# A planner that counts bank reads and stores, and an earlier first stage, in a hybrid gMLP and neighbourhood-attention block

## The chip, the cores and the metric

One core of a Trainium2 chip. The metric is device time in microseconds (us); lower is better.

## The reference

```python
S, D_MODEL, CHUNK, A_WIDTH, A_GROUPS = 2048, 1024, 128, 512, 4
B_HEADS, B_HEAD_DIM, GRID_W, WIN_ROWS_MAX, WIN_COLS, D_FF = 8, 64, 64, 8, 16, 4096
h = rms_norm(x, norm1_g)
proj = h @ w_in                                  # [u, v | q, k, av | gates a, b]
z_a = gelu(proj[..., :1024])
y_a = u * (einsum('gpq,bnqgc->bnpgc', w_s, layer_norm(v)) + b_s)
q, k = rms_norm(q, q_g) * hd ** -0.5, rms_norm(k, k_g)
y_b = attention of each of 32 x 64 grid cells over its 8 x 16 window, with bias rpb
gates = sigmoid(gate_pre + b_gate)               # 2 x 1024 columns
merged = gates[..., :1024] * (y_a @ w_o_a) + gates[..., 1024:] * (y_b @ w_o_b)
x = x + merged @ w_out
x = x + square(relu(rms_norm(x, norm2_g) @ w_ff1)) @ w_ff2
```

All is float32.

## The kernel before

Every product is made of three TensorE products of a high and a low part (hi and lo of both operands, without lo by lo), each 128x128 by 128x512. The large products go by a seven-product scheme: a unit takes sums of four blocks of weights (w_r, w_s and their hi and lo parts r and t; `w_seven`, L1377) and of rows (r1, r2, t23, t4) and makes 7 x 12 = 84 products (`seven`, L1447). They run in the order 1, 5, 6, 3, 7, 2, 4 over three banks of PSUM, z, x and y. ScalarE copies bank z after product 1 and 6 and bank x after 5 (`feat`, L330), and the next product that adds to the bank waits for that copy. GpSimd makes the sums (`sums`, L352, for rows; L1391 to L1401 for weights), ScalarE casts them (L1351, L1435), VectorE subtracts for the low part (L1355, L1439).

The rows are two halves h of 1024 tokens. `first_steps` (L1012) goes: `first_u` (L419), which makes u of h 0 by 192 whole products on the rows as loaded, with the mean square from squares on GpSimd (L408) and additions on VectorE (L414); eight units of gates of h 0; two units of u of h 1; eight units of gates of h 1; then values and queries of all rows, by slices that they load from DRAM (xf, `x_slice`). Beside these, `rows_out` (L540) loads rows of xT, scales them (L556), sums them and stores them to xf: four jobs for h 1 in units 2 to 5 of the first gates, four for h 0 in the first four units of the second gates. `first_w` (L574) does the same for the weights of values and queries. `bias_tables` (L935) builds the attention's bias on GpSimd's own DMA queue: 24 loads, three masks and 93 puts (L989), spread over gates and u. Attention, merge, output product and two up and down stages of the MLP follow, by units of the same kind.

The order on every engine is fixed ahead by a planner (`Plan.run`, L112). A step is TensorE work with a cost; a chain is a list of stages on SP, ScalarE, VectorE or GpSimd, each with a cost, a lead before the step that needs it, and the count of buffers (51 in all) that it takes or gives back. A stage is issued at the latest at its due step, and earlier where its engine's clock and the buffers allow. All stages of a chain that are due are issued at once, ready or not (`force`, L180), and what an engine was given runs in that order.

```python
while k < len(c.stages) and c.latest[k] <= i:
    k += 1
if k > c.done:
    force(c, k, i, t0)
```

## Time and profile before

| | |
|---|---|
| median of 3 runs | 2709.9 us (2708.07 to 2717.45) |
| the profiled execution | 2714.44 us |
| its span | 2712.6 us |
| its mean granted TensorE clock | 0.972 |
| DMA | 573.76 MB, 211 GB/s over the span |

The page gives busy time by engine: PE is TensorE's products, PEld its weight loads, DVE VectorE, ACT ScalarE, POOL GpSimd, SP the engine that issues most DMAs. A view by windows gives the same for a stretch of time, with the granted clock and the DMA share. A timeline row shows start and duration of an instruction, `out<-in`, and in square brackets how long its engine sat idle before it and what ended that. In the view of waits, a row names who waited for whom: total, times, longest.

### The profile page before, as it was taken

What the parts mean: (1) busy time and instruction counts of PE and PEld (TensorE: products, weight loads), DVE (VectorE), ACT (ScalarE), POOL (GpSimd) and SP (SyncE); (2) the same over time, 40 slices, a digit from 0 to 9 for tenths busy, and PEclk for the clock granted to TensorE, in tenths of its full rate; (3) what the DMA queues carried; (4) which work ended last, traced back from release to release, by engine and by line L of the source; (5) the groups of instructions that cost most, each with busy time, mean ns of one, the idle gap of its engine ahead of it and who ended that gap; (6) DMA issues with size and microseconds to landing.
All of it is one profiled execution on the core that took longest, in us unless ns stands there. A gap on an engine that the chain in (4) does not pass through costs nothing.

```text
span 2712.6 us, 34217 instructions
## 1 busy us (share of the span) xinstructions
PE 2535.4 (93%) x11820; PEld 2063.4 (76%) x11820; DVE 1831.4 (68%) x2593; ACT 1185.2 (44%) x1854; POOL 1136.2 (42%) x904
## 2 busy tenths in 40 slices
PE   7689699899998999999998999899998999989999
PEld 6577578687776777778886888778886888868887
DVE  6756556777887666663646666687877566678876
ACT  4455344665554555532334443433334444434341
POOL 6756568100000111132435766533432676734341
PEclk9899899999999999999998999899999999989999
DMA  5578878878778999986865444654346444474443
GB/s 163 161 244 235 283 246 290 318 211 250 207 197 214 306 322 323 328 310 217 283 223 177 152 153 144 212 193 166 133 147 233 152 152 148 147 263 144 157 142 113
DMA packets 402844, 573.76 MB, mean 212 GB/s; under 512 B 34477, under 2 KB 269396, under 8 KB 402672
## 3 DMA queue, kind: packets, MB, share of 16 engines
q1 hardware_dynamic: 389888, 557.65, 63.6%
q0 software_dynamic: 8640, 13.92, 1.9%
q8 instruction: 93, 1.52, 0.2%
q10 hardware_dynamic: 4144, 0.02, 0.1%
q14 instruction: 79, 0.65, 0.1%
HBM read 368.45 MB, written 202.98 MB: 211 GB/s over the span
## 4 chain that ended last, share of the span: by engine, by line
PE 70%; DMA 11%; DVE 7%; issue 3%; POOL 3%; ACT 2%; SPq 1%; DVEq 0%; POOLq 0%; ACTq 0%
PE z L1467 28%; PE x L1467 13%; PE fg L304 11%; PE y L1467 7%; PE z L640 4%; PE x L640 2%; DMA vw<-vs 1%; PE y L640 1%; PE s L1154 1%; DMA w<-in_xT_dram 1%; PE pv L1226 1%; PE pTp L1199 1%; DMA kst<-ks 1%; DVE x_r L1439 1%; DMA bias<-tb 1%
## 5 line engine op out<-in xcount | busy, mean ns | idle before, releaser
L1467 PE MATMUL z<-x_t,t_hi 128*128 128x512 f32 x1184 | 376.1, 399 | 60.2 <-ACT fe L330 25.9
L1355 DVE TENSOR_TENSOR r_lo<-w_r,r_hi 128x1024 fp32r<-128x1024 f32 (+3 forms) x176 | 280.9, 1597 | 107.3 <-ACT r_hi L1351 102.8
L1394 POOL TENSOR_TENSOR w_s<-w_r 128x512 f32<-128x512 f32 (+3 forms) x88 | 152.6, 1734 | 396.0 <-DVE x L1784 164.4
L1467 PEld LDWEIGHTS z<-x_t,t_hi 128*128 128x128 f32 x1184 | 226.3, 193 | 115.0 <-ACT fe L330 27.6
L1101 POOL CAST q<-qn 128x256 fp32r<-128x256 f32 x128 | 48.7, 423 | 588.6 <-DMA ks<-qo 337.9
L1467 PE MATMUL z<-x_t,t_lo 128*128 128x512 f32 x592 | 234.7, 396 | 0.9 <-DVE t_lo L1355 0.9
L1351 ACT CAST r_hi<-w_r 128x1024 fp32r<-128x1024 f32 (+3 forms) x176 | 173.8, 989 | 123.1 <-PE z L1467 47.0
L1467 PE MATMUL x<-x_r,t_hl 128*128 128x512 f32 x888 | 218.5, 394 | 1.9 <-DVE t_hl L1355 1.9
L1467 PEld LDWEIGHTS x<-x_r,t_hl 128*128 128x128 f32 x888 | 168.5, 190 | 38.5 <-DVE t_hl L1355 2.3
L1435 ACT CAST x_r<-x_r 128x1024 fp32r<-128x1024 f32 x104 | 107.4, 1049 | 201.5 <-PE x L1467 145.9
L1467 PE MATMUL z<-x_t,r_hi 128*128 128x512 f32 x592 | 184.6, 393 | 5.1 <-DVE a_B L1718 4.1
L1467 PE MATMUL z<-x_r,r_hi 128*128 128x512 f32 x592 | 183.9, 392 | 0.0
L1467 PE MATMUL y<-x_r,r_hi 128*128 128x512 f32 x592 | 183.5, 391 | 0.0
L1467 PE MATMUL x<-x_r,r_hi 128*128 128x512 f32 x592 | 182.2, 389 | 0.0
L304 PE MATMUL fg<-y,w_hi 128*128 128x512 f32 x512 | 162.2, 398 | 9.4 <-DMA y<-ya 5.9
L1400 POOL TENSOR_TENSOR w_s<-w_r 128x512 f32<-128x512 f32 (+3 forms) x88 | 162.3, 1844 | 3.4
L304 PE MATMUL fg<-mg,w_hi 128*128 128x512 f32 x512 | 158.0, 389 | 0.8 <-DVE mg L1540 0.8
L1439 DVE TENSOR_TENSOR x_r<-x_r,x_r 128x1024 fp32r<-128x1024 f32 x104 | 140.8, 1371 | 21.5 <-ACT x_r L1435 21.5
L1401 POOL TENSOR_TENSOR w_s<-w_r,w_s 128x512 f32<-128x512 f32 (+3 forms) x88 | 143.0, 1625 | 27.4 <-DVE r_lo L1355 11.1
L1355 DVE TENSOR_TENSOR t_lo<-w_s,t_hi 128x1024 fp32r<-128x1024 f32 (+3 forms) x88 | 135.1, 1535 | 17.3 <-ACT t_hi L1351 8.3
L1784 DVE TENSOR_TENSOR x<-z,x 128x512 f32<-128x512 f32 x152 | 104.7, 689 | 61.5 <-PE z L1467 60.9
L1467 PEld LDWEIGHTS z<-x_t,r_hi 128*128 128x128 f32 x592 | 112.0, 190 | 30.2 <-issue 4.8
(253 smaller groups left out, 5992.6 us busy)
## 6 DMA issues: line engine op xcount, KB each, us to landing
w_r<-in_w_ff_dram SPq DMA_DIRECT2D x116, 512.0 KB
x_r<-af SPq DMA_DIRECT2D x64, 512.0 KB
w_r<-in_w_in_dram SPq DMA_DIRECT2D x36, 512.0 KB
gt<-fe SPq DMA_DIRECT2D x32, 512.0 KB
x_r<-xf SPq DMA_DIRECT2D x32, 512.0 KB
qn<-qs SPq DMA_DIRECT2D x64, 256.0 KB
g<-gt SPq DMA_DIRECT2D x64, 256.0 KB
x<-x SPq DMA_DIRECT2D x32, 512.0 KB
```

The source lines that it names most:

```text
L304: self.nc.tensor.matmul(out, w[p], x[q], start=(i == 0 and j == 0), stop=(i == n - 1 and j == 2))
L640: nc.tensor.matmul(out, a[u], b[v], start=(p in (1, 5, 2) and k == 0 and j == 0), stop=(k == 3 and j == 2), skip_group_check=p in (6, 3, 7 ...
L1101: nc.gpsimd.tensor_copy(e[0][1][:, cb].rearrange("p l (r c) -> p (l r) c", c=16), e[1][1].rearrange("p l (r f c) -> p f (l r) c", f=4, c=1 ...
L1351: nc.scalar.copy(e[name + "_"][1][0], e[name][1])
L1355: nc.vector.tensor_tensor(lo, e[name][1], hi.bitcast(F32), ALU.subtract)
L1394: nc.gpsimd.tensor_tensor(s23[:, :, 1], r1[:, :, 0], r1[:, :, 1], ALU.subtract)
L1400: nc.gpsimd.tensor_tensor(s23[:, :, 0], r1[:, :, 1], r1[:, :, 0], ALU.subtract)
L1401: nc.gpsimd.tensor_tensor(e["t4"][1], r2[:, :, 0], s23[:, :, 0], ALU.subtract)
L1435: nc.scalar.copy(hi, lo.bitcast(F32))
L1439: nc.vector.tensor_tensor(lo, lo.bitcast(F32), hi.bitcast(F32), ALU.subtract)
L1467: nc.tensor.matmul(out, a[u], b[v], start=(p in (1, 5, 2) and k == 0 and j == 0), stop=(k == n - 1 and j == 2), skip_group_check=p in (6, ...
L1784: nc.vector.tensor_tensor(v, bank, v, ALU.add)
```

## The change

- `Stage` gets a lag: a store gives its buffers back 5 us after its step in the planner's count, and its cost falls from 3.0 to 1.6.
- Products 6, 3, 7 and 4 are, in the planner's clock, put behind the read of the bank by 1, 5, 6 and 7 (`behind`).
- A stage on ScalarE or VectorE that is due but not ready by the end of the step is put off by a step, where no step needs it yet and buffers allow (`put_off`).
- The squares in `first_u` go from GpSimd to ScalarE.
- The first unit of gates of h 0 is made in `first_u` by 96 whole products; the loop starts at unit 1, with `first_w` and `rows_out` one unit later.
- The rows of h 0 are stored to xf right after they are summed in `first_u`; the four jobs that loaded them again are gone, and `first_w(1)` goes to every other unit of the second gates.
- The bias tables start at the values and are due at the end of the queries, with 8 loads in place of 24. Each put waits for the eighth before it, as it did.

```diff
@@ -141,9 +146,11 @@
-                net[i + 1] += st.give
+                c.back.append(min(n, step_at(at[i + 1] + st.lag, i + 1)))
+                net[c.back[-1]] += st.give
...
@@ -184,6 +193,25 @@
+        def put_off(c, i, t):
+            k = c.done
+            if c.stages[k].eng not in ("ACT", "DVE") or i + 2 >= n or (c.first is not None and c.first <= i):
+                return False
+            if any(a.done < m for a, m in c.after) or max([c.ready] + [a.ends[m - 1] for a, m in c.after]) <= t:
+                return False
+            new = [(j, min(n, step_at(at[i + 2] + c.stages[j].lag, i + 2))) for j in range(k, len(c.stages)) if c.latest[j] <= i]
+            for j, b in new:
+                if any(free[x] < c.stages[j].give for x in range(c.back[j], b)):
+                    return False
+            for j, b in new:
+                for x in range(c.latest[j], i + 1):
...
+                c.latest[j], c.back[j] = i + 1, max(b, c.back[j])
+            return True
...
@@ -193,12 +221,10 @@
             for c in active:
-                k = c.done
-                while k < len(c.stages) and c.latest[k] <= i:
-                    k += 1
-                if k > c.done:
-                    force(c, k, i, t0)
-            now = max([now] + [c.ready for c in needs[i]])
+                while c.done < len(c.stages) and c.latest[c.done] <= i:
+                    if not put_off(c, i, t0 + s.cost + 0.3):
+                        force(c, c.done + 1, i, t0)
+            now = max([now] + [c.ready for c in needs[i]] + ([self.steps[s.behind].read] if s.behind is not None else []))
...
@@ -225,6 +251,7 @@
+            s.read = end + 0.2 if not s.costs else max(clock[e] for e in s.costs) + 0.1
...
@@ -404,17 +431,14 @@
-            if width == 512:
-                nc.gpsimd.tensor_tensor(o, x, x, ALU.mult)
...
+            nc.scalar.activation(o, x, AF.Square)
-        return self.plan.chain([Stage("ACT" if n == 2 else "POOL", 1.3 if n == 1 else 1.1, square, new, 0, 6, 0.3), Stage("DVE", 0.1 + 0.58 * n, add, 0, 0, 3, 0.3)], after)
+        return self.plan.chain([Stage("ACT", 0.1 + 0.5 * n, square, new, 0, 6, 0.3), Stage("DVE", 0.1 + 0.58 * n, add, 0, 0, 3, 0.3)], after)
...
@@ -513,6 +537,42 @@
+        wg = [self.w_cols(a["w_in"][0], (4 * r, 4 * r + 3), C_G, 12) for r in range(2)]
+        for m in range(2):
+            o = {}
...
+                        for k in ks:
+                            v = wg[k // 4][0]["w"][1]
+                            x = xs[k // 2]["r1" if k % 2 == 0 else "r2"][1]
+                            for j, (p, q) in enumerate(((0, 0), (0, 1), (1, 0))):
+                                nc.tensor.matmul(bank[0], v[p][:, k % 4, m * P : m * P + P], x[q][:, b], start=(k == 0 and j == 0), stop=(k == 7 and j == 2))
...
+                        nc.vector.tensor_tensor(v, bank[0], self.rows["in", 0, b], ALU.mult)
+                        nc.scalar.activation(v, v, AF.Sigmoid, bias=self.bg[:, m : m + 1])
...
+                    for q in range(4):
+                        ks = range(2 * q, 2 * q + 2)
+                        need = [wg[q // 2][1]] + [A[b, k] for k in ks]
+                        i = plan.step(6 * self.MM, lambda ks=ks: prod(ks), need, evac if q == 3 else None, int(b == 0 and q == 3), {"DVE": 0.7, "ACT": 0.7} if q == 3 else {})
...
+                last = gate()
...
+            self.gt_done[0, m] = (self.post(last, [self.store(st, 1, 0)], 8), 1)
...
@@ -523,17 +583,30 @@
+            def out(name, part, e=e, c=c):
+                def f():
+                    p0, p1 = self.X_PART[part]
+                    x = e.get("raw " + name, e[name])[1]
+                    for p in range(p0, p1):
+                        v = x[:, p - p0] if p1 - p0 == 2 else x
+                        nc.sync.dma_start(self.xf[0][:, :, p, c], v.rearrange("p (t q) -> p t q", q=P))
+                return f
...
+            o = {"r1": plan.chain([Stage("ACT", 0.6, cast, 0, 0, 5, 0.3), Stage("DVE", 0.7, sub, 0, 0, 2.7, 0.2)], af, start=last, hold=self.kept(e, "r1", 2)),
+                 "r2": plan.chain([Stage(None, 0, lambda: None, 0, 0, 12)], af, hold=self.kept(e, "r2", 2)),
+                 "t23": plan.chain(self.hilo(e, "t23", [2, 512], 3, False, True), af, hold=self.kept(e, "t23", 2)),
+                 "t4": plan.chain(self.hilo(e, "t4", [512], 3, True, True), af, hold=self.kept(e, "t4", 1))}
+            o["r1", 0] = A[0, 2 * c]
+            names = (("w2", "r2"), ("t23", "t23"), ("w1", "r1"), ("t4", "t4"))
+            st = plan.chain([Stage("SP", self.DMA if p != "t4" else 0.5 * self.DMA, out(nm, p), 0, 0, 4 - 0.5 * i, 1.0)
+                             for i, (nm, p) in enumerate(names)], af)
+            self.xf_done[0, c] = (st, 4)
+            for i, (nm, p) in enumerate(names):
+                def free(e=e, nm=nm):
+                    self.give(e.get("raw " + nm, e[nm])[0])
+                plan.chain([Stage(None, 0, free, 0, 1, 0)], ((st, i + 1), (o[p], len(o[p].stages))), due={"r2": -10, "r1": -2.7}.get(p, 0), like=o[p])
...
@@ -953,36 +1027,29 @@
+        for h in range(NH):
+            def t_load(h=h):
+                src = self.sk[h * 15 : (h + 1) * 15, 0 : 16 * TW]
+                src = src.rearrange("r (c w) -> c r w", w=TW)[:, :, off : off + w0]
+                g.dma_start(e["all"][h * 16 : (h + 1) * 16], src)
+            add(t_load)
         for ct, w in enumerate(KIND_W):
...
-                def t_load(h=h, off=off, w=w):
-                    src = self.sk[h * 15 : (h + 1) * 15, 0 : 16 * TW]
-                    src = src.rearrange("r (c w) -> c r w", w=TW)[:, :, off : off + w]
-                    g.dma_start(e["t"][h * 16 : (h + 1) * 16], src)
-                add(t_load)
...
+                k0 = 8 * (ct == 0)
...
+                g.tensor_tensor(e["t"], e["all"][:, :, k0 : k0 + w], e["c"][:, ct : ct + 1, :w].broadcast_to([P, 15, w]), ALU.add)
...
@@ -1005,7 +1072,7 @@
-        c = self.plan.chain([Stage("POOL", 1.0, f, t, gv, 5 + 2.2 * (n - i), 0.0) for i, (f, t, gv) in enumerate(fs)], start=start)
+        c = self.plan.chain([Stage("POOL", 2.0, f, t, gv, 5 + 2.2 * (n - i), 0.0) for i, (f, t, gv) in enumerate(fs)], start=start)
...
@@ -1026,12 +1093,13 @@
-            if c < 2:
-                self.first_w(0, c, len(plan.steps) + 5)
-            elif c < 6:
-                self.rows_out(1, c - 2, len(plan.steps) + 5, norm)
+            if c == 0:
+                continue
+            if c < 3:
+                self.first_w(0, c - 1, len(plan.steps) + 5)
+            elif c < 7:
+                self.rows_out(1, c - 3, len(plan.steps) + 5, norm)
...
@@ -1052,12 +1120,10 @@
         for c in range(8):
             i = len(plan.steps) + 5
-            end = i
-            if c < 4:
-                self.rows_out(0, c, i)
-            else:
-                self.first_w(1, c - 4, i)
+            if c % 2:
+                self.first_w(1, c // 2, i)
...
+        start = len(plan.steps)
-        self.bias_tables(start, end)
+        self.bias_tables(start, len(plan.steps))
...
@@ -1334,9 +1400,10 @@
     DMA = 1.6
+    LAG = 5.0
...
@@ -1468,16 +1538,16 @@
-            ids[p] = plan.step(3 * n * self.MM, mm, [w[1][wn]] + [x[1][xn] for x in xs],
-                               (lambda fn=fn, bank=bank: fn(banks[bank])), take, costs, free)
+            ids[p] = plan.step(3 * n * self.MM, mm, [w[1][wn]] + [x[1].get((xn, xi), x[1][xn]) for x in xs],
+                               (lambda fn=fn, bank=bank: fn(banks[bank])), take, costs, free, ids.get({6: 1, 3: 5, 7: 6, 4: 7}.get(p)))
-    def store(self, fn, give=0, lead=0.0, cost=3.0):
-        return Stage("SP", cost, fn, 0, give, lead, 0.0)
+    def store(self, fn, give=0, lead=0.0, cost=1.6):
+        return Stage("SP", cost, fn, 0, give, lead, 0.0, self.LAG)
```

On ScalarE, at the end of the first products, where the row of factors rs_row is copied out of PSUM for the second half of the tokens; r, t and w in casts of 128x512 and t_404 to t_472 are rows and their sums, w_r and w_s sums of weights, z the tile of u. Before:

```order
L521 CAST r_123<-w_121 128x512
L521 CAST r_141<-w_139 128x512
L521 CAST r_153<-w_151 128x512
L521 CAST r_171<-w_169 128x512
L1351 CAST t_hi<-t_404 128x1024
L1351 CAST t_hi<-t_457 128x1024
L1351 CAST t_hi<-t_472 128x1024
L1351 CAST t_hi<-t_469 128x1024
L1351 CAST t_hi<-w_s_340 128x1024
L1669 COPY rs_row<-rs_T 128x512
L494 ACT_TABLE_LOAD
L494 ACTIVATE z<-z 128x512 x4
```

After:

```order
L482 ACTIVATE w_151<-w_151,g_103 128x1024
L1418 CAST r_hi<-w_r_283 128x1024
L1418 CAST t_hi<-w_s_328 128x1024
L1739 COPY rs_row<-rs_T 128x512
L518 ACT_TABLE_LOAD
L518 ACTIVATE z<-z 128x512 x4
L1418 CAST t_hi<-t_547 128x1024
```

The four second-half casts of rows (L521) and the four casts of their sums no longer stand ahead of the copy; one cast of w_r and one of w_s are left there.

On ScalarE, in the first unit of gates of the second half, where fe<-z is the copy that frees bank z; w_2290 and w_2292 are rows of xT. Before:

```order
L1049 ACTIVATE fe<-fe 128x512
L1351 CAST t_hl<-w_s_2209 128x512
L556 ACTIVATE w_2290<-w_2290,g_103 128x1024
L556 ACTIVATE w_2292<-w_2292,g_103 128x1024
L330 COPY fe<-z 128x512
L330 COPY fe<-x 128x512
L1351 CAST r_hi<-w_r_2132 128x1024
L330 COPY fe<-z 128x512
```

After:

```order
L1418 CAST t_hl<-w_s_2150 128x512
L1117 ACTIVATE fe<-fe 128x512
L1418 CAST r_hi<-w_r_2076 128x1024
L357 COPY fe<-z 128x512
L357 COPY fe<-x 128x512
L1418 CAST r_hi<-w_r_2182 128x1024
L1418 CAST t_hl<-w_s_2267 128x512
L357 COPY fe<-z 128x512
L1418 CAST t_hi<-w_s_2245 128x1024
```

The two scalings of rows (L556) are gone from ahead of the copy, and the cast of r_hi that followed it now stands there.

On GpSimd, the start of the bias tables (tbx and tbi are their buffers, sk a strip in DRAM). Before, among the sums of weights and rows of the first gates:

```order
L1400 TENSOR_TENSOR w_s_702<-w_r_343 128x4x128
L1401 TENSOR_TENSOR w_s_727<-w_r_625,w_s_702 128x512
L946 MEMSET tbx 120x96
L947 DMA tbx<-in_na_rpb_dram 120x31
L950 DMA sk<-tbx 1920x1x96
L957 DMA tbx<-in_column_mask_dram 128x96
L364 TENSOR_TENSOR t_798<-w_627 128x512
L365 TENSOR_TENSOR w_627<-w_627,w_750 128x512
L373 TENSOR_TENSOR t_798<-w_627 128x512
L374 TENSOR_TENSOR t_820<-w_750,t_798 128x512
L973 DMA tbx<-sk 16x15x24 x8
L978 TENSOR_TENSOR tbx<-tbx 128x360
```

After, behind the last sums before values and queries:

```order
L400 TENSOR_TENSOR t_3129<-w_3014 128x512
L401 TENSOR_TENSOR t_3152<-w_3055,t_3129 128x512
L1020 MEMSET tbi 120x96
L1021 DMA tbi<-in_na_rpb_dram 120x31
L1024 DMA sk<-tbi 1920x1x96
L1031 DMA tbi<-in_column_mask_dram 128x96
L1041 DMA tbx<-sk 16x15x32 x8
L1047 TENSOR_TENSOR tbx<-tbx,tbi 128x360
L1049 MEMSET tbi 128x528
```

The tables' chain stands whole behind the last weights' sums, and one load for each head is made where there were three.

## Rows read from the trace of the kernel before

**Rows 1.** The page's first part: busy us, share of the span, instructions.

```profile
PE 2535.4 (93%) x11820; PEld 2063.4 (76%) x11820; DVE 1831.4 (68%) x2593; ACT 1185.2 (44%) x1854; POOL 1136.2 (42%) x904
```

**Rows 2.** Windows by stage: start:end and length in us, then as headed.

```profile
core 0: us, PE busy (x) PEld busy (x) DVE busy (x) ACT busy (x) POOL busy (x), PEclk, DMA share, GB/s
0.00:68.90 68.90, 53.77 (x216) 42.55 (x216) 45.14 (x55) 33.19 (x44) 43.58 (x39) 0.95 0.52 160
68.90:106.10 37.20, 22.41 (x85) 17.63 (x85) 33.94 (x27) 19.31 (x26) 29.91 (x18) 0.82 0.39 135
106.10:265.80 159.70, 144.03 (x614) 117.04 (x613) 95.50 (x104) 79.19 (x103) 101.73 (x104) 0.95 0.80 232
265.80:316.50 50.70, 41.37 (x173) 33.41 (x172) 36.76 (x36) 24.25 (x34) 30.72 (x31) 0.90 0.96 290
316.50:488.60 172.10, 154.97 (x673) 127.12 (x673) 89.47 (x87) 76.60 (x101) 125.28 (x115) 0.96 0.83 276
488.60:867.00 378.40, 346.49 (x1594) 280.18 (x1592) 304.73 (x625) 204.20 (x308) 2.88 (x8) 0.97 0.76 225
867.00:1160.00 293.00, 267.54 (x1924) 209.24 (x1925) 179.44 (x562) 162.17 (x466) 48.35 (x122) 0.98 1.06 321
```

**Rows 3.** Chain of waits in an undisturbed unit: start, us, what.

```profile
409.85 5.44 PE z L1467 x24
```

**Rows 4.** Timeline of PE, first products and first unit of gates.

```profile
39.25 1.87 PE L1647 MATMUL ms<-ones,acc 128*128 128x1 f32 x8 [4.39 <-DVE acc L414]
...
81.24 1.19 PE L1467 MATMUL z<-r,r_hi 128*128 128x512 f32 x2 [12.39 <-DVE z L493]
...
86.49 0.79 PE L1467 MATMUL x<-r,r_hi 128*128 128x512 f32 x2
```

**Rows 5.** Timeline of VectorE, first products.

```profile
16.95 0.68 DVE L414 TENSOR_TENSOR acc<-acc,sq 128x512 f32<-128x512 f32 x1
...
21.26 1.51 DVE L414 TENSOR_TENSOR acc<-acc,sq 128x512 f32<-128x512 f32 x1 [0.93 <-POOL sq L408]
```

**Rows 6.** Timeline of ScalarE, first unit of gates.

```profile
74.46 3.89 ACT L1351 CAST t_hi<-t 128x1024 fp32r<-128x1024 f32 x4 [6.02 <-POOL t L371]
...
79.20 0.58 ACT L1669 COPY rs_row<-rs_T 128x512 f32<-128x512 f32 x1
```

**Rows 7.** PE's waits: us in total, times, longest.

```profile
PE z L1467 <- ACT fe L330: 41.6, 10, 13.5
```

**Rows 8.** Timeline of PE, first products after three of these waits.

```profile
118.26 0.80 PE L1467 MATMUL z<-t_hi 128*128 128x512 f32 x1 [6.56 <-ACT fe L330]
...
280.03 1.22 PE L1467 MATMUL z<-x_t,t_hi 128*128 128x512 f32 x2 [8.79 <-ACT fe L330]
...
335.44 1.22 PE L1467 MATMUL z<-x_t,t_hi 128*128 128x512 f32 x2 [13.50 <-ACT fe L330]
```

**Rows 9.** Timeline of ScalarE before these copies.

```profile
117.62 0.59 ACT L330 COPY fe<-z 128x512 f32<-128x512 f32 x1 [7.12 <-DMA gt<-fe]
...
275.62 3.88 ACT L1435 CAST x_r<-x_r 128x1024 fp32r<-128x1024 f32 x4 [4.56 <-DMA x_r<-xf]
...
332.53 2.38 ACT L556 ACTIVATE w<-w,g 128x1024 f32<-128x1024 f32 x2 [9.35 <-DMA w<-in_xT_dram]
```

**Rows 10.** The page's third part: GpSimd's queue, packets, MB, share.

```profile
q0 software_dynamic: 8640, 13.92, 1.9%
```

**Rows 11.** The tile tb: durations of its issues in ns, and time to landing.

```profile
L989 POOL DMA_DIRECT2D tb<-tbi x72: 597/598/637, 130.7 to 475.8; - x72
...
DMA to landing us min/median/max: 3.0/7.1/11.6
```

**Rows 12.** Windows of 20 us with much traffic, columns as in rows 2.

```profile
260.00:280.00 20.00, 11.24 (x54) 9.06 (x52) 14.20 (x14) 12.24 (x16) 10.82 (x15) 0.86 1.09 296
480.00:500.00 20.00, 16.05 (x63) 12.45 (x61) 15.35 (x15) 9.31 (x11) 6.40 (x5) 0.91 1.04 396
```

**Rows 13.** Timeline of PE, at the border of the second up stage.

```profile
2393.42 1.19 PE L1467 MATMUL z<-x_t,t_hi 128*128 128x512 f32 x2 [8.30 <-DVE x L1784]
```

More of the change, by code (lines that the diff above doesn't have):

```diff
@@ L60, with __init__ @@
 class Stage:
-    def __init__(self, eng, cost, run, take=0, give=0, lead=0.0, wait=0.0):
+    def __init__(self, eng, cost, run, take=0, give=0, lead=0.0, wait=0.0, lag=0.0):
         self.eng, self.cost, self.run, self.take, self.give, self.lead, self.wait = eng, cost, run, take, give, lead, wait
+        self.lag = lag
 class Chain:
@@ L92, in __init__, with step @@
         self.nbuf, self.steps, self.chains = nbuf, [], []
-    def step(self, cost, mm, need=(), evac=None, take=0, costs=(), free=None):
+    def step(self, cost, mm, need=(), evac=None, take=0, costs=(), free=None, behind=None):
         i = len(self.steps)
         self.steps.append(Step(cost, mm, evac, take, dict(costs), free or 0))
+        self.steps[i].behind = behind
         for c in need:
@@ L102, in step, with chain @@
         return i
-    def chain(self, stages, after=(), start=None, due=None, hold=None):
+    def chain(self, stages, after=(), start=None, due=None, hold=None, like=None):
         c = Chain(stages, after)
-        c.start, c.due, c.hold = start, due, hold
+        c.start, c.due, c.hold, c.like = start, due, hold, like
         self.chains.append(c)
@@ L123, in run @@
         for c in self.chains:
-            due = at[c.first] if c.first is not None else at[n] if c.due is None else at[min(n, c.start + 1)] + c.due
+            if c.like:
+                due = at[c.like.first] + c.due
+            else:
+                due = at[c.first] if c.first is not None else at[n] if c.due is None else at[min(n, c.start + 1)] + c.due
             c.low = min(c.start + 1 if c.start is not None else 0, n - 1)
@@ L169, in issue @@
             b = max(c.begin(), clock.get(st.eng, 0.0), t)
-            clock[st.eng] = b + st.cost
+            if st.eng:
+                clock[st.eng] = b + st.cost
             c.ready = max(c.ready, b + st.cost + st.wait)
@@ L174, in issue @@
                 free[j] -= st.take
-            for j in range(i + 1, c.latest[k] + 1):
-                free[j] += st.give
+            if st.give:
+                for j in range(min(n, step_at(at[i + 1] + st.lag, i + 1)), c.back[k]):
+                    free[j] += st.give
             st.run()
@@ L186, in force @@
                 issue(c, i, t)
+        def put_off(c, i, t):
[10 more added lines that the diff above has]
+                for x in range(c.latest[j], i + 1):
+                    free[x] += c.stages[j].take
+                for x in range(c.back[j], b):
+                    free[x] -= c.stages[j].give
+                c.latest[j], c.back[j] = i + 1, max(b, c.back[j])
+            return True
         self.log = []
@@ L567, in out @@
             return f
-        st += [Stage("SP", self.DMA, out(nm, p), 0, 1, 3 - 0.5 * i, 2.0) for i, (nm, p) in enumerate((("w1", "r1"), ("w2", "r2"), ("t23", "t23"), ("t4", "t4")))]
+        st += [Stage("SP", self.DMA, out(nm, p), 0, 1, 3 - 0.5 * i, 2.0, self.LAG) for i, (nm, p) in enumerate((("w1", "r1"), ("w2", "r2"), ("t23", "t23"), ("t4", "t4")))]
         ch = plan.chain(st, tuple(after))
@@ L941, in bias_tables @@
         add = lambda f, take=0, give=0: fs.append((f, take, give))
+        w0, off = 32, 39
         def v_load():
-            e["x"] = self.take([1024], F32, "tbx")
-            e["v"] = e["x"][1][:120, 480 : 480 + TW]
+            e["x"], e["y"] = self.take([1024], F32, "tbx"), self.take([1024], F32, "tbi")
+            e["v"] = e["y"][1][:120, 800 : 800 + TW]
             g.memset(e["v"], 0.0)
@@ L1336, with hilo @@
     DMA = 1.6
+    LAG = 5.0
     POOL, MM = 1.5, 0.2267
[L1339 removed]
+    def hilo(self, e, name, shape, lead, pair=False, keep=False):
         nc = self.nc
@@ L1470, in seven @@
             fn, take, costs, free = evac[p]
-            ids[p] = plan.step(3 * n * self.MM, mm, [w[1][wn]] + [x[1][xn] for x in xs],
-                               (lambda fn=fn, bank=bank: fn(banks[bank])), take, costs, free)
+            ids[p] = plan.step(3 * n * self.MM, mm, [w[1][wn]] + [x[1].get((xn, xi), x[1][xn]) for x in xs],
+                               (lambda fn=fn, bank=bank: fn(banks[bank])), take, costs, free, ids.get({6: 1, 3: 5, 7: 6, 4: 7}.get(p)))
         w[2].first = ids[1]
```

54 lines of the change are left out of this document (27 added, 27 removed).

## The prediction

> **What bounds the kernel now.** The page's busy line comes first: the reader is to see that TensorE works 93% of the span [rows 1], so that the most that any re-ordering can give back is the 177 us in which it stands still, unless products go away, and here 12 are added. Next the busy time by stage [rows 2]: the seven rows are the first products (A, 0 to 68.9 us), the first unit of gates (B, to 106.1), seven further units (C, to 265.8), two units of u of the second half (D, to 316.5), eight units of gates of the second half (E, to 488.6), values and queries (to 867.0), and attention (to 1160.0). In A to E, the stages that the change rewrites, 488.6 us hold 416.5 us of PE work: 72.1 of the 177 us stand there. Then the chain of waits through an undisturbed unit gives the price of work [rows 3]: 24 products take 5.44 us, 0.2267 each, so the 84 of a unit take 19.04. Against that a stage's loss is its length less its units at 19.04. Last come the timelines of PE, ScalarE and VectorE and PE's own waits, for what ends the idle time.
>
> **First products (A).** PE waits 4.39 us for the sum of squares [rows 4]. That sum is fed by 16 squares on GpSimd, and VectorE's addition of 128x512 takes 1.51 us beside GpSimd where another took 0.68 [rows 5]. The squares go to ScalarE. A 128x512 copy there takes 0.58 [rows 6], so 16 cost some 9.3 us, and ScalarE is busy 33.2 of A's 68.9 us: it has the room. A long wait also costs speed behind it: after one of 12.39 us, 12 products took 5.25 us, from 81.24 to 86.49, where 2.72 is the full price [rows 4, 3], so 2.5 on top. Bounds 0 and 6.9 (4.39 + 2.5). I take 6, near the upper end, because a wait of 4.39 is what these rows show and ScalarE has no other late work there.
>
> **First unit of gates (B).** It takes 37.2 us with a granted clock of 0.82 [rows 2]. PE waits 12.39 us in it, because ScalarE sat 6.02 us until GpSimd's sums t came, then cast for 5 us, and only then copied the row of factors [rows 6, 4]. The change computes this unit by 96 whole products on the rows themselves, so that the sums are not needed yet. The order shows the four casts of t gone from in front of that copy. New length: a wait of 2.0 for the factor row, 96 x 0.2267 = 21.8, and 4 at the end, for the second-half casts of r, which now wait for the last whole product. Behind it stand a multiplication and a sigmoid, then a cast (0.7, 0.6 and 0.6 by the nearest rows [rows 5, 6]) and a subtraction of up to 1.5, with the steps from engine to engine. Together 27.8. Gain **9.4**, net of 12 x 0.2267 = 2.7 for the added products. Bounds: 11.4 without the first wait, and 0 if the sums (GpSimd 29.9 of 37.2 us busy in B) are now waited for behind it.
>
> **Copies behind unready casts (C, D, E).** The largest wait in PE's list is for the copy that frees the z bank: 41.6 us in 10 waits [rows 7]. In C one lasts 6.56, at 118.26 [rows 8]. ScalarE's row tells why: it sat 7.12 before that copy, for a store of an earlier tile whose buffer was to be used again [rows 9]. In E the longest, 13.50, starts with ScalarE idle for 9.35 until a load of xT came, then two scalings of 2.38 together, then the copy [rows 8, 9]. Three edits bear on it: a cast that isn't ready by the end of its step is put off by a step; a product waits in the planner's clock for the read of its bank; and stores give their buffers back 5 us later in the planner's count, so that it no longer hands out a buffer whose store is under way. C takes 159.7 us for 7 x 19.04 = 133.3 and 2.9 for its small products: 23.5 lost. The scalings of xT for the second half still stand ahead of some copies there, and 28 stores of the first half's rows come before weight loads in SP's queue. So I keep 7 as lost: gain **16.5**, bounds 0 (the wait moves but stays) and 23.5. D takes 50.7 for 38.1 and 0.6: 12.0 lost, 8.79 of it in one wait for a copy that stood behind four casts of x_r, for whose load ScalarE had sat 4.56 us [rows 8, 9]. Its DMA share is 0.96 [rows 2], full, and stays so, since the same rows and weights must come. I take **2.5**, bounds -5 and 12.
>
> **First rows stored at once (E).** The four jobs that loaded xT again, scaled it, summed and stored it go: 8 loads of 512 KB, 8 scalings, 16 GpSimd sums. Their stores, 28 of 256 KB, move to the end of A. E takes 172.1 for 152.3: 19.8 lost, and the wait of 13.50 with its 2.5 of half speed is 16.0 of it. Its cause leaves the stage, and the order shows the two scalings gone from before the copy. First_w(1), spread over odd units, also loads and stores there, so I keep 2: gain **17.8**, bounds 13.5 and 19.8.
>
> **Bias tables.** Their 72 and 21 puts move from 130 to 480 us into values and queries, GpSimd's empty stage (2.9 us busy). GpSimd itself hides them: nothing there waits for it. They are done some 240 us before attention reads them. What is not hidden is traffic: the software queue moved 13.92 MB [rows 10]. With 8 in flight and 7.1 us from issue to landing, the 93 puts and 8 loads need 101 / 8 x 7.1, about 90 us, at 11.6 us 146 [rows 11]. That is 13.92 MB in 90 us, an estimate of 155 GB/s on top of the stage's 225. A window near that sum is in the trace: 480 to 500 moved 396 GB/s [rows 12]. I take **-3**: cost between 0, if slack takes it, and -13, if PE idled as in attention, 25.5 of 293.0 us at 321 GB/s [rows 2], for all 146 us. The Trainium skill, in "DMA: Bandwidth & Descriptors", section Specifications, puts a core's share of memory bandwidth at about 358 GB/s; by that 380 would leave 2.0 MB late, some 5.5 us, an estimate, instead of 3. The row with 396 GB/s disagrees with it, and the row decides.
>
> **The rest** keeps its products and their order; at the borders of the up and down stages some casts change places. The longest wait there lasts 8.30 [rows 13], with 2.5 of half speed 10.8. Two such taken away would give some +20, and one or two shorter ones added cost up to -15. Nothing in the order favours either, so 0. The store's lower cost (3.0 to 1.6) is a planner's number alone, with no instruction behind it: 0.
>
> **Sum.** 6 + 9.4 + 16.5 + 2.5 + 17.8 - 3 = 49.2 us. The profiled execution took 2714.4, so 2665.2; the median of the runs is 4.5 lower, so **2661**. Less than 0.3%, 8 us, can't be told from no change.
>
> **Rivals.** *All the losses of A to E go*: 6.9 + 11.4 + 23.5 + 12.0 + 19.8 = 73.6, and the tables cost nothing: 2636. For it: DMA has room over the first 106 us (shares 0.52 and 0.39). Against: D stays full.
>
> *The waits in C and D only move*: the planner changes who stands in front of the copy, but loads still come when buffers and DMA allow (share 0.80 and 0.96). Then 19 of the 49.2 are missing: 2680. For it: ScalarE's idle times before the late copies end with a DMA, not with an engine, and putting a cast behind a copy delays the weights of the next unit.
>
> *Slower: the tables starve the loads of values and queries.* The place is 489 to 635 us. PE is 92% busy there, fed by x slices and weights at 225 GB/s. If the packets of the tables, small and many, hold up those loads as D's first loads were held up (260 to 280 us, PE busy 11.24 of 20 [rows 12]), 44% of up to 146 us go: 64 on top, 2725. It decides from 39% idle over all of it. Against: beside the puts in C, PE was 90% busy. The Trainium skill, same page, section "Queues, rings and completion order", says that each DMA engine takes turns between the queues that have work for it, packet by packet; by that rule the tables' queue would get its turn ahead of a deep SP queue, which is this rival's mechanism. No row here shows the turns.
>
> **How the numbers follow.** Forecast 0.60, with a range of its own of 2647 to 2677: from all of C's bound upward to half of C gone. All losses go 0.12. Waits only move 0.16. Tables starve fully 0.06 (slower), in part 0.06, at 2690 to 2718, of which 0.04 within 0.3%. The low end takes in the first rival, 2636; the high end, 2690, the second with its spread; out are the third and thin tails. Faster 0.60 + 0.12 + 0.16 + 0.02 = 0.90, same 0.04, slower 0.06.
>
> **What would show it.** Right: PE's wait for the z copies falls from 41.6 to under 15; no wait over 5 us in the first gates; E takes under 156 us and C under 145; values and queries take 378 to 385. Wrong: copies that still follow idle times ended by DMA in C; a new wait at the end of the whole products, for r or t; a values stage over 400 us with loads of x landing late; a TensorE clock under 0.9 anywhere after 110 us.

## The result and the profile after

The changed kernel takes 2738.07 us (median of 4 runs, 2733.52 to 2740.49), the kernel before 2713.51 beside it. The ratio is 1.009, with a 95% interval from 1.0064 to 1.0116: slower by 25 us, where 2661 was forecast.

The windows by stage of the changed kernel, columns as in [rows 2]: first products, first unit of gates, seven units, u of the second half, second gates, values and queries up to the first product of attention, attention.

```profile
0.00:64.70 64.70, 52.07 (x216) 41.38 (x216) 37.89 (x57) 42.52 (x59) 17.63 (x18) 0.95 0.58 179
64.70:90.20 25.50, 23.50 (x97) 19.33 (x97) 12.96 (x14) 12.42 (x16) 17.82 (x13) 0.93 0.86 256
90.20:243.80 153.60, 143.36 (x614) 115.27 (x612) 91.63 (x106) 80.97 (x107) 70.69 (x49) 0.97 0.83 253
243.80:298.20 54.40, 44.37 (x177) 34.96 (x176) 42.47 (x38) 25.90 (x35) 33.48 (x20) 0.91 0.68 228
298.20:450.50 152.30, 152.22 (x670) 125.60 (x671) 90.08 (x94) 72.83 (x98) 60.27 (x40) 1.00 0.65 222
450.50:885.70 435.20, 361.25 (x1602) 289.46 (x1600) 299.46 (x619) 200.62 (x305) 71.83 (x122) 0.92 0.76 213
885.70:1180.00 294.30, 270.76 (x1904) 211.41 (x1903) 175.89 (x559) 160.16 (x463) 45.47 (x120) 0.95 1.05 310
```

Values begin at 450.5 us instead of 488.6: the first stages gained 38.1. The second gates run without a wait, 152.22 us of PE in 152.30. Then values and queries take 435.2. The kernel before, cut at the same place, takes 380.0:

```profile
488.60:868.60 380.00, 348.09 (x1602) 281.78 (x1600) 305.28 (x625) 204.69 (x309) 3.01 (x9) 0.97 0.76 225
```

55.2 us are lost there, more than all that was gained. From attention to the end it is 1853.0 us against 1844.0. PE's waits of the changed kernel (us in total, times, longest) name the place: PE waits until VectorE and ScalarE have copied the values out of PSUM. The waits for fe of [rows 7], 41.6 us before, are no longer among the largest (3.0).

```profile
PE z L713 <- DVE av L757: 20.7, 4, 9.8
PE x L713 <- ACT av L745: 18.8, 3, 8.9
...
PE z L713 <- ACT vg L745: 10.1, 1, 10.1
```

Neither engine is the cause, as the chain of waits shows (start, us, what; SPq is SP issuing a DMA, L677 the load of a slice, L845 a store of av):

```profile
519.51 2.50 SPq L677
522.05 14.47 DMA x_t<-xf
...
536.54 0.59 SPq L845
...
554.62 10.84 DMA ya<-ya
...
565.49 0.86 SPq L677
...
606.29 14.88 DMA x_t<-xf
...
621.20 0.29 SPq L845
...
638.64 5.79 DMA x_r<-xf
```

The chain runs through the casts and products of a slice to the store of its result ya, and from there to the next load, which SP issued when the store had landed (565.49). The two loads of 14.47 and 14.88 us, 512 KB each, are on the chain in another way. SP had issued seven stores of av behind each of them, and it issued the next one, the eighth DMA after the load, when the load had landed (536.54 and 621.20). So a slow landing holds up SP's queue, and with it every load that stands behind. A load of 512 KB issued after the last put landed in 5.79 us. The 16 stores of av of one slice took SP 16.64 to 21.25 us beside the puts, and 7.17 to 10.32 in the changed kernel without tables (an experiment below). One row of each:

```profile
566.44 21.25 SPq L845 DMA_DIRECT2D vs<-av  x16
```

```profile
564.27 7.46 SPq L845 DMA_DIRECT2D vs<-av  x16
```

What shares the DMA engines meanwhile is told by the DMA queues of the changed kernel from 560 to 640 us (packets, MB, share of 16 engines):

```profile
q1 hardware_dynamic: 10354, 9.47, 42.3%
q0 software_dynamic: 4537, 7.56, 37.4%
```

and by that of the kernel before in the same stretch:

```profile
q1 hardware_dynamic: 16843, 15.48, 68.1%
```

SP's queue moved 9.47 MB instead of 15.48 while GpSimd's took 37.4% of the engines. The tile tb says when: all 93 puts within 109 us (durations in ns, first and last start), where the kernel before spread them over some 345 [rows 11].

```profile
L1056 POOL DMA_DIRECT2D tb<-tbi x72: 594/596/635, 514.4 to 622.2; - x72
L1056 POOL DMA_DIRECT2D tb<-tbx x21: 596/596/612, 515.0 to 622.8; - x21
```

The loss lies in that stretch. Its window in the changed kernel, and then the same stretch in the changed kernel without tables:

```profile
514.40:622.80 108.40, 65.69 (x261) 53.35 (x262) 44.92 (x80) 32.14 (x44) 58.41 (x99) 0.77 0.81 215
```

```profile
514.60:623.00 108.40, 99.81 (x470) 82.64 (x469) 71.81 (x126) 56.51 (x76) 0.00 (x0) 0.98 0.65 194
```

PE made 261 products there instead of 470. At the 0.2267 us of [rows 3], 209 products are some 47 us. It stood still for 39% of the stretch, and the granted clock was 0.77.

### The profile page after: what moved, and what is told of

It reads as the page before. It is cut to its first block, busy times and chain, and to the rows that moved or that the text cites. A ratio compares the mean times of both kernels' runs of the same rounds, so it can differ in the third digit from the quotient of the medians.

```text
span 2738.7 us, 34122 instructions
## 1 busy us (share of the span) xinstructions
PE 2553.1 (93%) x11832; PEld 2074.2 (76%) x11832; DVE 1810.2 (66%) x2588; ACT 1181.1 (43%) x1857; POOL 1103.9 (40%) x852
## 4 chain that ended last, share of the span: by engine, by line
PE 69%; DMA 13%; DVE 9%; SPq 3%; ACT 2%; issue 2%; POOL 1%; ACTq 0%; DVEq 0%; POOLq 0%
PE z L1537 30%; PE x L1537 15%; PE fg L331 11%; PE y L1537 7%; DMA vw<-vs 2%; DMA x_t<-xf 2%; SPq L845 1%; PE z L713 1%; DMA x_r<-xf 1%; DVE x_r L1509 1%; PE fg L502 1%; PE pv L1292 1%; DMA y<-ya 1%; DMA bias<-tb 1%; PE x L713 1%
## 5 line engine op out<-in xcount | busy, mean ns | idle before, releaser
L1422 DVE TENSOR_TENSOR r_lo<-w_r,r_hi 128x1024 fp32r<-128x1024 f32 (+3 forms) x174 | 254.2, 1463 | 83.1 <-ACT r_hi L1418 83.1
L1509 DVE TENSOR_TENSOR x_r<-x_r,x_r 128x1024 fp32r<-128x1024 f32 x104 | 147.4, 1436 | 20.7 <-ACT x_r L1505 20.7
L1422 DVE TENSOR_TENSOR t_lo<-w_s,t_hi 128x1024 fp32r<-128x1024 f32 (+3 forms) x87 | 136.7, 1572 | 19.7 <-DMA af<-a_D 11.5
L1471 POOL TENSOR_TENSOR w_s<-w_r,w_s 128x512 f32<-128x512 f32 (+3 forms) x87 | 133.6, 1535 | 25.4 <-DVE t_lo L1422 7.8
L1537 PEld LDWEIGHTS z<-x_r,r_hi 128*128 128x128 f32 x592 | 113.2, 192 | 29.6 <-DVE x_r L1509 5.8
```

Of the source, the lines that this page charges most:

```text
L1422: nc.vector.tensor_tensor(lo, e[name][1], hi.bitcast(F32), ALU.subtract)
L1471: nc.gpsimd.tensor_tensor(e["t4"][1], r2[:, :, 0], s23[:, :, 0], ALU.subtract)
L1509: nc.vector.tensor_tensor(lo, lo.bitcast(F32), hi.bitcast(F32), ALU.subtract)
L1537: nc.tensor.matmul(out, a[u], b[v], start=(p in (1, 5, 2) and k == 0 and j == 0), stop=(k == n - 1 and j == 2), skip_group_check=p in (6, ...
```

## The experiments

Theory T: the tables' traffic holds up the loads of values, and moving the tables there is the whole loss. Rival S: the planner's new rules or the moved stores slow the values. Stage marks of the profiled executions, in us; "v+q" reaches to the first product of attention, "time" is the median of the runs. The kernel before was timed again beside each set, at 2713.5 to 2719.2, so that costs between sets are taken from the ratios, times 2713.5. By their intervals a difference of two ratios is good to some 6 us, or 8 where the changed kernel's 1.009 is one of them. A stage mark is from one execution.

| kernel | values begin | v+q | time | ratio to before (95%) |
|---|---|---|---|---|
| before | 488.6 | 380.0 | 2713.5 | |
| changed | 450.5 | 435.2 | 2738.1 | 1.009 (1.0064 to 1.0116) |
| before, tables at the values | 454.9 | 422.2 | 2731.8 | 1.0061 (1.0046 to 1.0077) |
| changed, tables in gates, count 2.0 | 496.7 | 386.3 | 2739.7 | 1.0106 (1.0087 to 1.0125) |
| changed, tables in gates, count 1.0 | 482.4 | 391.3 | 2723.1 | 1.0018 (1.0003 to 1.0032) |
| before, no tables | 456.9 | 376.8 | 2685.9 | 0.9883 (0.9865 to 0.9901) |
| changed, no tables | 450.7 | 385.9 | 2687.8 | 0.9885 (0.9869 to 0.9901) |
| changed, an eighth of the bytes | 446.7 | 385.9 | 2694.7 | 0.9916 (0.99 to 0.9932) |
| changed, paced puts | 448.9 | 423.7 | 2722.5 | 1.0023 (1.0013 to 1.0033) |
| changed, puts on SP | 446.9 | 411.5 | 2711.9 | 0.9986 (0.997 to 1.0002) |
| changed, tables in second gates | 471.1 | 394.3 | 2715.8 | 0.9997 (0.9985 to 1.001) |
| changed, second gates into values | 449.8 | 397.2 | 2697.8 | 0.9929 (0.9912 to 0.9947) |
| before, second gates into values | 476.3 | 399.8 | 2723.6 | 1.0019 (1.0006 to 1.0031) |
| changed, second gates into values, no lag | 453.2 | 407.5 | 2706.5 | 0.9955 (0.9942 to 0.9969) |

**The tables moved alone, on the kernel before** (with the changed table function and its count of 2.0):

```diff
-        self.bias_tables(start, end)
+        self.bias_tables(start, len(plan.steps))
...
+        start = len(plan.steps)
         for p, f in ((0, self.values), (1, self.queries)):
```

> The kernel before with one edit: the changed kernel's table function, started at the values. Theory T: values and queries grow from 378 to 420 to 440 us, gates and u lose nothing or gain up to 10, whole 2745 to 2770. Rival S: values and queries stay within 10 us of 378, whole 2700 to 2720.

Values and queries grew by 42.2, as T has it. That gates and u would shrink by 33.7 us no theory said, so the whole, 2731.8, came out below T's range: in its first stages the kernel before gets most of the changed kernel's gain by losing the tables alone.

**The tables moved back, on the changed kernel**, start at the first gates, due at the second:

```diff
+        start = len(plan.steps)
         for c in range(8):
...
+            end = i
             gates(1, xs, c)
-        start = len(plan.steps)
...
-        self.bias_tables(start, len(plan.steps))
+        self.bias_tables(start, end)
```

> The changed kernel with one edit: the bias tables start at the first gates and are due at the second gates, as before. Theory T (the tables' traffic starves the loads of values): values and queries fall from 434 us to 378 to 390, gates and u grow by up to 15 us with the puts beside them, whole 2685 to 2710. Rival S (the planner's new rules or the order of stores make the values slow): values and queries stay at 425 us or more, whole 2730 or more.

Values and queries fell to 386.3: T. But the first stages grew by 46.2, three times what was expected. The timeline of PE shows a wait for r_hi at the start of each of the eight units of the second gates, 2.38 to 2.47 us long:

```profile
373.05 0.73 PE L1538 MATMUL z<-x_r,r_hi 128*128 128x512 f32 x2 [2.47 <-ACT r_hi L1419]
```

On ScalarE the casts of weights stood behind the last unit's four sigmoids: the planner, told 2.0 us for each table job, held GpSimd to be full and issued the weights at their due step. So the next run took the old count.

```diff
-        c = self.plan.chain([Stage("POOL", 2.0, f, t, gv, 5 + 2.2 * (n - i), 0.0) for i, (f, t, gv) in enumerate(fs)], start=start)
+        c = self.plan.chain([Stage("POOL", 1.0, f, t, gv, 5 + 2.2 * (n - i), 0.0) for i, (f, t, gv) in enumerate(fs)], start=start)
```

> The changed kernel with the tables in the gates and with the old count of 1.0 us for each of their jobs in the planner. With 2.0 (the run with tables in the gates) the weights' casts came at their due step, and PE waited 2.47 us in each unit of the second gates. If that count was the cause, these waits go, values begin at 475 to 488 us, and the whole is 2700 to 2716. If the tables' traffic alone was the cause, values begin at 493 or later and the whole is 2725 or more.

The waits of 2.47 us went (two shorter ones, of 1.75 and 1.53, are left) and values begin at 482.4, within what was expected. The whole, 2723.1, is 7 us above it, and values and queries are 5 us longer than without tables. With the tables in the gates, the changed kernel is no faster than before.

**No tables**, in both kernels; the bias loads read as many bytes elsewhere:

```diff
-        self.bias_tables(start, len(plan.steps))
+        self.bias_done = self.ut_done[1][-1]
...
-                    src = self.tb[ct][kind][2 * pair : 2 * pair + 2].rearrange("h r c k -> (r c) h k")
+                    src = self.ut[:P, : 2 * w].rearrange("p (h k) -> p h k", h=2)
```

> The changed kernel without bias tables: nothing of them is built, and the bias loads read as many bytes of another tensor (the bias is left out of the result). Theory T: gates and u end at 450 us as in the changed kernel, values and queries take 378 to 388, whole 2680 to 2695. Rival S: values and queries 410 or more, whole over 2715.

> The kernel before without bias tables (the bias is left out of the result). Theory T2 (the tables cost about as much beside the gates as beside the values, and the other edits give little): gates and u end at 450 to 460 us instead of 488.6, whole 2672 to 2688, no slower than the changed kernel without tables. Rival (the planner's edits and the early stores gave the 38 us of the first stages): they end at 475 or later, whole 2700 or more.

2687.8 and 2685.9: no difference that these runs can show. All the other edits together give nothing here, and the tables cost the changed kernel 56 us (1.009 less 0.9885) and the kernel before 32 (1 less 0.9883). Values and queries of the changed kernel without tables:

```profile
450.70:836.60 385.90, 350.55 (x1602) 282.26 (x1600) 299.69 (x619) 200.89 (x305) 4.26 (x12) 0.97 0.71 207
```

The other reads of the bias may have a price of their own. From attention to the end these two kernels take 1854.8 and 1857.1 us, and the next one, which reads the bias otherwise too, 1857.1. All the kernels that read the full tables take 1844.0 to 1853.0. So the costs from whole times may be some us too low. By the stage marks up to attention alone, the tables cost 49 us in the changed kernel and 35 in the kernel before.

The windows of the kernel before without tables, the seven units and the second gates, columns as in [rows 2]:

```profile
105.90:247.80 141.90, 137.40 (x613) 112.44 (x612) 98.08 (x104) 79.03 (x103) 65.96 (x44) 1.00 0.78 235
```

```profile
303.00:456.90 153.90, 152.17 (x669) 125.03 (x669) 92.95 (x88) 73.99 (x98) 89.49 (x60) 1.00 0.78 262
```

and its wait for fe:

```profile
PE z L1467 <- ACT fe L330: 10.3, 8, 4.1
```

The second gates take 153.9 us with all four jobs that load xT again, and 31.3 of the 41.6 us of that wait are gone with no edit to the planner.

**Bytes or issues.** The same 93 puts with an eighth of the bytes; the loads of the bias read that eighth twice:

```diff
-                    g.dma_start(self.tb[ct][kind][:, rq, :, k0 * w : (k0 + r1 - r0) * w],
-                                e[which][:, r0:r1, :].rearrange("p r k -> p (r k)"))
+                    g.dma_start(self.tb[ct][kind][0, rq, :, k0 * w : (k0 + r1 - r0) * w],
+                                e[which][:16, r0:r1, :].rearrange("p r k -> p (r k)"))
...
-                    src = self.tb[ct][kind][2 * pair : 2 * pair + 2].rearrange("h r c k -> (r c) h k")
-                    nc.sync.dma_start(e[0][1], src)
+                    src = self.tb[ct][kind][0:1].rearrange("h r c k -> (r c) h k")
+                    nc.sync.dma_start(e[0][1][:, 0:1], src)
+                    nc.sync.dma_start(e[0][1][:, 1:2], src)
```

> The changed kernel, whose 93 puts write one head of eight, and whose bias loads read that head (the bias of seven heads is left out): as many DMAs from GpSimd with an eighth of the bytes and packets. Theory T by bytes: values and queries 378 to 392 us, whole 2680 to 2698. Theory T by the number of DMAs or their issue: values and queries over 410, whole over 2715.

385.9 us, as without tables: bytes, not issues. Packets fell with the bytes, so these two aren't told apart. The cost left in the whole, 0.9916 less 0.9885, is 8 of 56 us, about a seventh and hardly more than the error.

**Pace.** Each put behind a GpSimd read of the newest tile of the stage, where `pace` is the last tile av or q that was copied out of PSUM, and 3.5 us for each job in the planner:

```diff
+                    if self.pace is not None:
+                        g.tensor_copy(e["y"][1][:, 900:901], self.pace[1][:, self.pace_b, 0:1])
                     g.dma_start(self.tb[ct][kind][:, rq, :, k0 * w : (k0 + r1 - r0) * w],
```

> The changed kernel, whose puts are spread over values and queries: each put stands behind a read of the newest tile of the stage, and the planner counts 3.5 us for it. Theory T: the same bytes at a third of the rate cost little, values and queries 378 to 395 us, whole 2680 to 2700. Rival S: values and queries 425 or more, whole 2730 or more.

A miss: 423.7, with the puts spread over 364 us, so 11.5 of 49 us saved. But the run doesn't price pace alone. Its longest wait of PE, 17.70 us, comes with the tables' start, by way of the new read: VectorE had to leave half a tile av alone until GpSimd had read it (L1065), and that read stood on GpSimd behind the start of the tables.

```profile
484.79 4.75 PE L713 MATMUL z<-x_r,x_t 128*128 128x512 f32 x12 [17.70 <-DVE av L759]
```

```profile
483.95 0.69 DVE L759 TENSOR_TENSOR av<-z,av 128x512 f32<-128x512 f32 x1 [18.12 <-POOL tbi L1065]
```

Up to the first put, in 31.7 us of values, PE made 73 products, where the changed kernel made 130 in its first 30.0. The difference is some 13 us at the 0.2267 of [rows 3]. The chain and SP's timeline there:

```profile
450.27 16.82 DMA sk<-tbi
```

```profile
455.62 9.45 SPq L677 DMA_DIRECT2D x_t<-xf  x1
```

**A queue of its own, or SP's.** The same puts issued by SP, in the planner's order with SP's loads:

```diff
-                    g.dma_start(self.tb[ct][kind][:, rq, :, k0 * w : (k0 + r1 - r0) * w],
+                    nc.sync.dma_start(self.tb[ct][kind][:, rq, :, k0 * w : (k0 + r1 - r0) * w],
...
-        c = self.plan.chain([Stage("POOL", 2.0, f, t, gv, 5 + 2.2 * (n - i), 0.0) for i, (f, t, gv) in enumerate(fs)], start=start)
+        c = self.plan.chain([Stage("SP" if i in sp else "POOL", 0.6 if i in sp else 2.0, f, t, gv, 5 + 2.2 * (n - i), 0.0) for i, (f, t, gv) in enumerate(fs)], start=start)
```

> The changed kernel, whose 93 puts are issued by SP in its own order, 0.6 us each in the planner's count, in place of GpSimd's software queue; the same bytes in the same stages, spread over values and queries. Theory Q (a queue of its own takes turns with SP's and holds up its loads): values and queries fall from 435 to under 405 us, whole under 2710. Theory B (the bytes alone, beside loads whose landing is on the path of each slice): values and queries stay at 420 or more, whole 2720 or more.

411.5, between the two: 24 us saved, half of the cost. The puts also lie over 276 us instead of 109, so queue and pace aren't told apart by it. The paced run beside it (364 us, own queue, 423.7) doesn't help: less the 13 us of its start it would come to about 411 as well, an estimate. Whether a queue of its own has a share in the cost stays open. Even from SP's queue and at this pace the puts cost 26 us (411.5 less 385.9).

**Beside a stage with room.** In the changed kernel the second gates leave the DMA engines at 0.65.

```diff
+        first = len(plan.steps)
         for c in range(8):
             i = len(plan.steps) + 5
...
-        self.bias_tables(start, len(plan.steps))
+        self.bias_tables(first, start)
...
-        c = self.plan.chain([Stage("POOL", 2.0, f, t, gv, 5 + 2.2 * (n - i), 0.0) for i, (f, t, gv) in enumerate(fs)], start=start)
+        c = self.plan.chain([Stage("POOL", 1.0, f, t, gv, 5 + 1.3 * (n - i), 0.0) for i, (f, t, gv) in enumerate(fs)], start=start)
```

> The changed kernel with the tables beside the eight units of second gates alone (planner cost 1.0, due spread by 1.3 us, due at the values). PE ran there without a wait and DMA share was 0.65 in the changed kernel; the tables need about 51 us of all 16 engines, so some 0.98 with them. Theory B with slack (the bytes cost only where landing is on the path or the engines are full): gates and u end at 455 to 470, values and queries at 386 to 392, whole 2692 to 2712. If each byte costs the same everywhere, gates and u end at 482 or later and the whole is 2718 or more.

And the same with an end 30 steps later and 2.0 in place of 1.3:

```diff
-        self.bias_tables(first, start)
+        self.bias_tables(first, start + 30)
```

> The same, but spread by 2.0 us from the start of the second gates to some 70 us into the values. Theory B with slack: a third of the bytes falls on the values and costs a third of 49 us there, gates lose less than 8 us, whole 2705 to 2720, slower than with the second gates alone. If even spreading is what counts, it is the faster of the two, under 2700.

The first missed: values begin at 471.1, and the wait of 2.47 us for r_hi is back in two units. A likely reason is that the planner has too many table jobs due for the weights' sums to come early; that was not tried alone. The second, expected to be the slower one, is the fastest of all that build the tables: **2697.8 us, 0.9929 of the kernel before (0.9912 to 0.9947)**, 44 us less than the change as it stands (1.009 less 0.9929). Its windows, second gates and then values and queries:

```profile
298.00:449.80 151.80, 150.02 (x658) 122.83 (x657) 91.68 (x89) 66.01 (x91) 109.97 (x118) 1.00 0.86 261
449.80:847.00 397.20, 357.10 (x1602) 285.75 (x1600) 303.08 (x622) 206.28 (x309) 23.48 (x42) 0.95 0.75 219
```

Most puts lie in the second gates (the last starts at 489.9), DMA share rises from 0.65 to 0.86, and PE loses nothing there. The tables cost 12 us in all, give or take 6 (0.9929 less 0.9885), and 10 by the stage marks. Between the two runs pace and end changed together, so which of them did it is open.

**The same place on the kernel before** (with the changed table function, count 1.0 and 2.0 us apart), whose second gates still hold the four jobs:

```diff
-        self.bias_tables(start, end)
+        self.bias_tables(first, start + 30)
```

> The kernel before with the tables placed as in the run spread from the second gates into the values (new table function, planner cost 1.0, due spread by 2.0 us). Its second gates carry the four jobs that load, sum and store the first rows again, which the changed kernel has left out. If the early stores are what makes room for the tables there, PE waits return in the second gates, values begin at 465 or later, and the whole is 2705 to 2720, slower than 2697.8. If place and pace of the tables are all, values begin at 455 to 460 and the whole is 2690 to 2700.

2723.6, 24 us slower (1.0019 less 0.9929) than the same tables in the changed kernel: values begin at 476.3, and their first slices come late.

```profile
360.21 1.22 PE L1461 MATMUL z<-x_t,t_hi 128*128 128x512 f32 x2 [7.11 <-ACT fe L330]
```

```profile
512.10 1.22 PE L640 MATMUL z<-x_t,x_t 128*128 128x512 f32 x2 [18.48 <-ACT vg L672]
```

So the other edits, which give nothing without tables, give the room for them. Which of these edits does so was not tried.

**Without the lag of stores**, on the fastest version:

```diff
-    LAG = 5.0
+    LAG = 0.0
```

> The run spread from the second gates into the values, with the lag of stores set to 0. Without tables the changed kernel takes 9 us more in values and queries than the kernel before. If the lag is the cause (loads wait in the planner for buffers), values and queries fall from 397 to 390 or less and the whole is 2686 to 2694. If the lag keeps loads from waiting for stores in flight, they stay or grow and the whole is 2697 to 2712.

2706.5, 7 us slower (0.9955 less 0.9929), just beyond the error, with values and queries at 407.5 instead of 397.2. With the tables at this place the lag doesn't make values slower; it seems to help. Without tables it was not tried.

## Why the prediction was wrong

**The step that failed** is the term for the tables, -3 with bounds of 0 and -13. Measured: 435.2 less 385.9, 49 us. The estimate of time under traffic was near (about 90 us; the puts took 109), but the bound was not: it took attention's 9% idle as the most that full DMA can do to PE. Beside the puts the DMA engines were not full (a share of 0.81, against 0.65 without tables) and moved little more than without them (215 and 194 GB/s), and still PE stood idle for 39% of the stretch. The chain that feeds PE goes through landing times and through SP's queue, one after another. Loads of 512 KB took 14.47 and 14.88 us beside the puts and 5.79 after them, and the store of ya, 512 KB as well, took 10.84. Of the 49 us, 10.7 are not waits but the products themselves (PE busy 361.25 and 350.55 us), at a granted clock of 0.92 instead of 0.97. The store of ya in the changed kernel without tables:

```profile
535.09 3.56 DMA ya<-ya
```

**The rival that named it** was "the tables starve the loads of values and queries": mechanism and place hold, and the size nearly (64 on top), but it had 0.12 in both strengths. It gave 44% of up to 146 us idle, and 39% of 108 was measured. Its "small" packets don't hold: from 560 to 640 us those of the tables had 1.7 KB (7.56 MB in 4537), those of SP's queue 0.9 (9.47 MB in 10354). Against it stood that PE was 90% busy beside the puts in C. That was misread: without them it is 97% there (137.40 of 141.90). The rule of the Trainium skill's "DMA: Bandwidth & Descriptors", section "Queues, rings and completion order", that each DMA engine takes turns between the queues that have work for it, fits q0's 37.4% beside q1's 42.3%; these are shares of 80 us, and no trace here shows the turns. The 358 GB/s of the same page's section Specifications would have given 5.5 us, by the estimate in the prediction, a ninth of what was measured.

**C and E.** The gain in E was forecast as 17.8 and measured as 19.8, but not for the reason given: the number was right by luck. The wait of 13.50 us ended with a load of xT, and the load was late because of the tables. SP issued it 7.6 us after E began, and without tables, with the four jobs still there, 8.6 us ahead of it, so that the same load and scalings cost PE nothing. The kernel before, and then the same without tables (E from 303.0):

```profile
324.07 1.82 SPq L1369 DMA_DIRECT2D w<-in_xT_dram  x2
```

```profile
294.38 0.93 SPq L1369 DMA_DIRECT2D w<-in_xT_dram  x2
```

Ahead of the late load the chain goes through slow issues on SP (four in 8.13 us at 299.05), a load of weights and GpSimd's sums. Whether the tables held these up by their traffic or by their time on GpSimd, where the sums stand among the puts, is not told apart for the gates. In C the tables had cost 17.8 us (159.7 less 141.9; 142.1 with them moved to the values). The two terms of 34.3 us were put to the planner's order and the early stores; they belonged to the move that was priced at -3. The chain names the instruction that came last, not who slowed it.

**A and B** were right in size: 4.2 and 11.7 us against 6 and 9.4. In B the products took PE 23.5 us, 1.7 more than said, and the waits took less. **C** gave it back: forecast at a gain of 16.5, it gained 6.1, and that only because the tables left it. It takes 153.6 us in the changed kernel, 152.1 without tables, against 141.9 in the kernel before without tables. Of its waits, 10.2 us, more than half are for the low parts of weights (r_lo, 5.5), at a DMA share of 0.83 with the 28 stores now ahead. That these stores are the cause was not tried alone.

**D** was forecast at +2.5 and came out 3.7 longer, inside its bounds. Values and queries are 9.1 us longer in the changed kernel even without tables (385.9, 376.8). Which edit does that is open. From attention to the end the kernels with full tables took 1844 to 1853 us, with nearly the same code there; the two at hand are the ends of that range, and the 9 us between them, forecast as 0, were not explained. "No difference" from the other edits was thus a sum of gains in A and B and losses in C and values.

Of the signs that the prediction named, E came out under 156 us, but C not under 145, and two signs of being wrong came: values over 400 us with loads landing late, and a clock under 0.9 after 110 us (0.77 beside the puts). Its own range doesn't follow from what it names: all of C's bound is 7 us up and half of C 8 down, and the ends stand 14 and 16 away.

## What to carry to other kernels

A background transfer is priced by the stage beside it. As the chains here read, what counts is not the mean DMA share but whether a landing time is a link of the chain that feeds the bound engine, be it directly or through the queue of the engine that issues the loads; loads issued further ahead were not tried. The same tables, some 13.5 MB, cost 56 us beside values, 32 in the kernel before, spread over gates and u, and 12 mostly beside a stage where PE ran without a wait (49, 35 and 10 by the stage marks). Before a wait is put to an order, run the kernel without the suspected neighbour: that run here took away 31 of 41.6 us that the chain had put to loads and scalings. And a read that is added to pace a transfer is a new link itself, as PE's wait of 17.70 us shows.

## What the runs showed of the hardware

The store sk<-tbi writes 1920 rows of 96 elements. In the paced run it took 16.82 us to land, and during it one issue on SP lasted 9.45 us, where the two after the next took 0.32. In the changed kernel, where that store starts at 495.2, SP's 16 stores of av from 493.85 on took 12.71 us, and 7.75 a slice earlier. There, too, two issues of vs<-av at 524.62 took 5.54 us beside the puts:

```profile
524.62 5.54 SPq L845 DMA_DIRECT2D vs<-av  x2
```

A planner's count for a job off the bound engine has a price, though no instruction stands behind it: 2.0 instead of 1.0 us for each table job moved the values' start by 14.3 us (496.7 and 482.4).
